# Eight weight sums and a page's sum moved from VectorE to GpSimd in the first two column groups of an encoder layer, and its third score tile issued two plain steps later

## The chip, the cores and the metric

The kernel runs on one core of a Trainium2 chip. Its engines are TensorE (PE; the loading of its stationary operand is listed as PEld), VectorE (DVE), ScalarE (ACT), GpSimd (POOL) and SyncE (SP), which here issues the DMA transfers. The metric is the device time of one execution in microseconds (us); lower is better.

## The reference, cut to what matters

One layer of an encoder over 2048 tokens of width 1024, in float32:

```python
h = rms_norm(x, norm_mix)
z = h @ w_in                       # 1024 x 4352: q_a k_a v_a q_b k_b v_b gate_a gate_b
y_a = windowed_gqa(q_a, k_a, v_a, sink)       # window 128, ALiBi, 8 heads over 2 KV heads
y_b = neighborhood_attn(q_b, k_b, v_b, rpb)   # 8 x 16 neighbourhood on a 32 x 64 grid
x = x + (sigmoid(g_a + b_a) * (y_a @ w_proj_a) + sigmoid(g_b + b_b) * (y_b @ w_proj_b)) @ w_out
x = x + square(relu(rms_norm(x, norm_mlp) @ w_up)) @ w_down
return rms_norm(x, norm_final)
```

The change touches the start of `h @ w_in` and the start of the windowed attention.

## The kernel before

**Number format.** Every large product is made of three matmuls (lines 313 to 315, and 203 to 205 in a later stage). An operand is split into a high part, rounded to the matmul format, and the rest: ScalarE casts the high part (L309) and VectorE subtracts it from the source (L310). An operand is ready for L313 when its high part is there, for L314 or L315 when the rest is.

**The first stage.** Tokens are taken in four pages of 512. The product of the first two pages with `w_in` goes by a Strassen scheme: a group of columns is cut into four quarters `a11, a12, a21, a22` (two halves of the columns, two halves of the 1024 inputs), the two token pages likewise, and seven products per group (numbers 1, 2, 5, 6, 7, 4, 3 in `ORDER`) replace eight. Products 5, 6 and 3 need sums of weight quarters first: `s1 = a21 + a22`, `a21 = a11 - a21`, `s2 = a22 - a21`, `a12 = a12 - s2`. They need sums of token pages too (`zraw` tiles t1 and t3 hold them, made from the pages `zh1`, `zh2`). `in_left` (L398) yields the weight operand of each product; `add` (L304) is the helper that makes every sum; `left_parts` splits the result into a `zwhl` tile.

**The start.** Each of the eight 128-token tiles `xin` is normalised: ScalarE and VectorE sum the squares (L236, L238), VectorE joins them (L241), GpSimd raises the result to the power -1/2 (L242), VectorE multiplies (L559 for the first page, L577 for the second), TensorE transposes (L301) into PSUM, and from PSUM ScalarE and VectorE write the scaled high part and rest (L534, L537). Column group 0 (`quad0`, weights in `kvw` tiles, 128 columns a quarter) and group 1 (`quad1`, weights in `zraw` tiles, 256 columns a quarter) run through the same stretch, and the page sum `t1 = zh1 high + zh1 rest` (two instructions of 128x1024) is made there too. The sums `s1` and `s2` of both groups share a ring of two `zS` buffers: the third `zS` waits until the split of the first is done, the fourth until that of the second is.

**What sets the order.** Python code issues the instructions, and a scheduler of the framework places them on each engine's queue; `tc.issue_after(x)` keeps an instruction behind `x` in that order. Each queue is worked off in its order, and waits on semaphores where a value comes from elsewhere (or, on GpSimd, from its own instruction just before).

**The attention's start.** `Unit.score` issues two matmuls of a score tile (L821) into one of two PSUM buffers `s`; VectorE adds the bias `biasa` and reads the tile out (L825). Between the score tiles of the first units run "plain steps", three matmuls each of the column tiles of the other two token pages. The table `FIRST` says how many plain steps precede each score tile: (0, 2), the third tile, stands at 14 and (1, 0) at 16.

Of the kernel before, what the change touches and what calls it, by code (L numbers as in the profile page):

```python
# [8 lines left out]
F32 = mybir.dt.float32  # L9
F32R = mybir.dt.float32r  # L10
AF = mybir.ActivationFunctionType
ALU = mybir.AluOpType
# [10 lines left out]
P = 128  # L23
# [72 lines left out]
def encoder_layer(ctx, tc, x, norm_mix, w_in, b_gate, sink, rpb, w_pa, w_pb, w_out,  # L96
# [41 lines left out]
    power = cr.tile([P, 1], F32, name="power")  # L138
# [83 lines left out]
            if k < KC - 1:  # L222
                yield "step"

    last_dma = [None]

    def load_tile(pl, tag, bufs, rows):
        t = T(pl, [P, D], F32, tag, bufs)
# [3 lines left out]
    def rstd_shared(pl, t):  # L232

        st = T(pl, [P, 4], F32, "st", 4)
        junk = T(pl, [P, 512], F32, "junk", 1)
        A.activation(junk, t[:, 0:512], AF.Square, accum_out=st[:, 0:1])  # L236
        other = T(pl, [P, 512], F32, "junkv", 1)
        V.tensor_tensor_reduce(out=other, in0=t[:, 512:1024], in1=t[:, 512:1024], scale=1.0, scalar=0.0,  # L238
                               op0=ALU.mult, op1=ALU.add, accum_out=st[:, 1:2])
        r = st[:, 2 : 3]  # L240
        V.scalar_tensor_tensor(out=r, in0=st[:, 0:1], scalar=D * EPS, in1=st[:, 1:2], op0=ALU.add, op1=ALU.add)  # L241
        G.tensor_tensor(out=r, in0=r, in1=power, op=ALU.pow)  # L242
        return r

    def rstd_of(pl, t, jp=None, mean=False):
# [57 lines left out]
    def add(eng, out, a, b, op=ALU.add):  # L303
        return eng.tensor_tensor(out=out, in0=a, in1=b, op=op).ins  # L304
# [90 lines left out]

    last_part, last_low = [None], [None]

    def in_left(ws, w, skip=(), behind=None):  # L398

        a11, a21 = ws[0][:, :, 0:w], ws[0][:, :, w : 2 * w]  # L400
        a12, a22 = ws[1][:, :, 0:w], ws[1][:, :, w : 2 * w]

        def parts(src, eng):
            return left_parts(src, w, eng)

        s1, s2 = None, None
        for n in ORDER:
            if n in skip:
                continue
            with tc.issue_after(behind[0]) if behind else nullcontext():  # L410
                if n == 5:
                    s1 = in_sum()[:, :, 0:w]
                    add(V, s1, a21, a22)
                elif n == 6:
                    add(V, a21, a11, a21, ALU.subtract)
                    s2 = in_sum()[:, :, 0:w]
                    add(V, s2, a22, a21, ALU.subtract)
                elif n == 3:
                    add(V, a12, a12, s2, ALU.subtract)
            yield parts({1: a11, 2: a12, 5: s1, 6: s2, 7: a21, 4: a22, 3: a12}[n], V)  # L420

    def v_parts(col, b, vt, p2, v2):
# [139 lines left out]
    for k in range(KC):  # L562
# [2 lines left out]
        h, l = (t[:, k % 4] for t in right[1 + k // 4])  # L565
        scaled(h, ps, k)
        last_low[0] = scaled_less(l, ps, k, h.bitcast(F32)).ins
    sums0, sums1 = [last_low[0]], [None]
    t1, t3 = in_raw(), in_raw()

    quad0 = in_quad(*QUADS[0], in_left(ws0, P, behind=sums0), right, xpool[1:], xpool[:1])
    quad1 = in_quad(*QUADS[1], in_left(ws1, 256, behind=sums1), right)
    next(quad0)
    next(quad0)
    sums1[0] = last_low[0]
    for n, t in enumerate(tiles[1]):
        V.tensor_scalar(t, t, rstd_shared(xp, t), float(D) ** 0.5, ALU.mult, ALU.mult)  # L577
    next(quad1)
# [9 lines left out]
    for p in range(2):  # L588
        t = T(xp, [P, D], F32, "xin", 8).rearrange("p (k c) -> p k c", k=4)
        c = QUADS[2][0]  # L590
        SY.dma_start(t, w_in[0][p * BT : (p + 1) * BT, c : c + 256].rearrange("(k p) f -> p k f", p=P))
        ops2.append(left_parts(t, 256, V))
        if p == 0:
            with tc.issue_after(last_part[0]):
                for o, h, l in zip(halves(t1), *map(halves, right[1])):
                    add(V, o, h.bitcast(F32), l.bitcast(F32))
        next(quad2)
    for n in (5, 3, 6):
        right[n] = (in_page[n](), in_page[n]())
# [309 lines left out]
        load_kv(g, 0)  # L909
    units = [Unit(g, i) for g in (1, 0) for i in range(7)] + [Unit(g, i) for g in range(2) for i in range(7, 16)]  # L910
    AHEAD, PLAIN, SCORE, STEP = 3, 24 * KC, 0.27, 0.68
    FIRST = {(0, 2): 14, (1, 0): 16, (1, 2): 18, (2, 0): 20, (2, 2): 22, (3, 0): 24}

    def prepare(n):
        if n + 2 < len(units):
# [853 lines left out]
```

## Time and profile before

| what | value |
|---|---|
| median of 3 runs | 2587.47 us (2585.76 to 2590.54) |
| the profiled execution's own time | 2589.41 us |
| its span | 2587.6 us, 34569 instructions |
| granted TensorE clock, mean | 0.999 |
| GpSimd (POOL) | 366.9 us busy (14%), 493 instructions |
| GpSimd between 28 and 66 us | 0 us busy |
| DMA over the span | 189 GB/s |

The page gives for each engine the busy time within one profiled execution. Rows of the timeline read: start and length in us, engine, line, operation, output and inputs, shape, count; in brackets the idle time of the engine before it and what ended that. In the profile VectorE's row at 26.20 us, for example, is the split L310 of a 128x1024 weight tile. A row that joins several instructions ("x4") shows the length of all of them.

### The profile page before, as it was taken

How to read it: one execution, taken by the hardware profiler on the slowest of the kernel's cores; microseconds unless marked ns; L12 is line 12 of the kernel's file. 1: busy time of each engine (PE TensorE's matmuls, PEld its weight loads, DVE VectorE, ACT ScalarE, POOL GpSimd, SP SyncE). 2: the span in 40 equal slices, each digit the busy share in tenths (PEclk: the TensorE clock that was granted, in tenths of full speed). 3: DMA queues.
4: the chain of work that ended last, by engine and by line, in shares of the span. 5: the costliest groups of instructions: out<-in, count | busy, mean ns of one | idle time of the engine just before them, and what ended most of it. 6: DMA issues, size and time to landing. Idle time of an engine off the chain costs nothing.

```text
span 2587.6 us, 34569 instructions
## 1 busy us (share of the span) xinstructions
PE 2562.3 (99%) x12140; PEld 2142.1 (83%) x12140; DVE 1608.8 (62%) x2621; ACT 1234.9 (48%) x2261; POOL 366.9 (14%) x493
## 2 busy tenths in 40 slices
PE   8999999999999999999999999999999999999999
PEld 6888778888888888888888888888888888888887
DVE  8866656765544444665578767866666535554766
ACT  5334347776565556443335554654454322323454
POOL 1000024455555541000000000100000000000010
PEclk9999999999999999999999999999999999999999
DMA  5657486476967646775456666844428835445555
GB/s 186 205 155 208 124 253 182 126 191 186 232 190 196 190 138 227 230 220 167 134 179 230 232 210 212 305 162 164 153 101 314 281 100 183 144 154 163 187 195 172
DMA packets 354126, 490.39 MB, mean 190 GB/s; under 512 B 28808, under 2 KB 188808, under 8 KB 351776
## 3 DMA queue, kind: packets, MB, share of 16 engines
q1 hardware_dynamic: 346896, 471.14, 58.6%
q10 hardware_dynamic: 7056, 17.04, 1.8%
q8 instruction: 96, 1.57, 0.3%
q14 instruction: 78, 0.64, 0.1%
HBM read 328.64 MB, written 159.45 MB: 189 GB/s over the span
## 4 chain that ended last, share of the span: by engine, by line
PE 94%; DVE 3%; DMA 2%; ACT 1%; issue 1%; SPq 0%; POOL 0%; POOLq 0%; DVEq 0%; ACTq 0%
PE b L313 16%; PE b L315 16%; PE b L314 16%; PE mm L205 6%; PE mm L203 6%; PE mm L204 6%; PE zb L313 3%; PE zb L315 3%; PE zb L314 3%; PE pt L203 2%; PE pt L204 2%; PE pt L205 2%; PE av L1088 2%; PE pt L1067 2%; PE s L1036 2%; PE pt L843 2%
## 5 line engine op out<-in xcount | busy, mean ns | idle before, releaser
L314 PE MATMUL b<-dwh,dah 128*128 128x512 f32 x896 | 348.5, 389 | 0.0
L315 PE MATMUL b<-dwh,dah 128*128 128x512 f32 x896 | 347.6, 389 | 0.0
L313 PE MATMUL b<-dwh,dah 128*128 128x512 f32 x896 | 339.6, 389 | 0.0
L309 ACT CAST dah<-da 128x1024 fp32r<-128x1024 f32 (+1 forms) x128 | 120.9, 945 | 368.9 <-PE b L315 241.8
L310 DVE TENSOR_TENSOR dah<-da,dah 128x1024 fp32r<-128x1024 f32 (+1 forms) x128 | 139.4, 1089 | 222.6 <-ACT dah L309 218.3
L314 PE MATMUL b<-ubh,uwhlb 128*128 128x512 f32 x592 | 230.3, 389 | 0.0
L313 PE MATMUL b<-ubh,uwhlb 128*128 128x512 f32 x592 | 230.2, 389 | 0.0
L315 PE MATMUL b<-ubh,uwhlb 128*128 128x512 f32 x592 | 229.2, 389 | 0.0
L203 PE MATMUL mm<-hT,whl 128*128 128x512 f32 x544 | 217.9, 401 | 0.4 <-DVE zc L304 0.4
L205 PE MATMUL mm<-hT,whl 128*128 128x512 f32 x544 | 213.5, 393 | 0.0
L204 PE MATMUL mm<-hT,whl 128*128 128x512 f32 x544 | 213.0, 391 | 0.0
L314 PEld LDWEIGHTS b<-dwh,dah 128*128 128x128 f32 x896 | 168.2, 188 | 35.0
L315 PEld LDWEIGHTS b<-dwh,dah 128*128 128x128 f32 x896 | 168.2, 188 | 34.9
L313 PEld LDWEIGHTS b<-dwh,dah 128*128 128x128 f32 x896 | 168.2, 188 | 34.9
L313 PE MATMUL zb<-zh,zwhl 128*128 128x512 f32 x476 | 186.5, 394 | 6.1 <-DVE st L253 2.0
L314 PE MATMUL zb<-zh,zwhl 128*128 128x512 f32 x476 | 186.5, 392 | 0.0
L315 PE MATMUL zb<-zh,zwhl 128*128 128x512 f32 x476 | 183.5, 391 | 1.8 <-DVE zwhl L310 1.8
L304 DVE TENSOR_TENSOR uc<-b,uc 128x512 f32<-128x512 f32 x160 | 109.0, 688 | 103.3 <-PE b L315 102.4
L1639 POOL TENSOR_TENSOR st<-st,power 128x1 f32<-128x1 f32 x16 | 13.4, 843 | 925.2 <-DVE st L1638 925.2
L313 PEld LDWEIGHTS b<-ubh,uwhlb 128*128 128x128 f32 x592 | 111.1, 188 | 23.4 <-issue 0.4
L314 PEld LDWEIGHTS b<-ubh,uwhlb 128*128 128x128 f32 x592 | 111.1, 188 | 23.2
L315 PEld LDWEIGHTS b<-ubh,uwhlb 128*128 128x128 f32 x592 | 111.1, 188 | 23.0
(262 smaller groups left out, 5839.5 us busy)
## 6 DMA issues: line engine op xcount, KB each, us to landing
at<-uc SPq DMA_DIRECT2D x224, 256.0 KB
da<-at SPq DMA_DIRECT2D x96, 512.0 KB
dw<-in_w_down_dram SPq DMA_DIRECT2D x160, 256.0 KB
uraw<-in_w_up_dram SPq DMA_DIRECT2D x32, 1024.0 KB
raw<-in_w_in_dram SPq DMA_DIRECT2D x34, 512.0 KB
zraw<-in_w_in_dram SPq DMA_DIRECT2D x16, 1024.0 KB
z<-zg SPq DMA_DIRECT2D x64, 256.0 KB
zg<-zc SPq DMA_DIRECT2D x32, 256.0 KB
```

What stands on the lines that cost most here:

```text
L203: PE.matmul(ps, lh, rh, start=first, stop=False)
L204: PE.matmul(ps, lh, rl, start=False, stop=False)
L205: return PE.matmul(ps, ll, rh, start=False, stop=last).ins
L304: return eng.tensor_tensor(out=out, in0=a, in1=b, op=op).ins
L309: casts.append(A.copy(hi, src).ins)
L310: return eng.tensor_tensor(out=lo, in0=src, in1=hi.bitcast(F32), op=ALU.subtract).ins
L313: PE.matmul(ps, lh, rh, start=first, stop=False, skip_group_check=True)
L314: PE.matmul(ps, lh, rl, start=False, stop=False, skip_group_check=True)
L315: PE.matmul(ps, ll, rh, start=False, stop=last, skip_group_check=True)
L843: ins = PE.transpose(pt[:, u * P : (u + 1) * P], self.s[:, u, c * P : (c + 1) * P], ident).ins
L1036: ins = PE.matmul(ps[:, :n], self.q[:, i, :], kv[:, z, B_R0[i] // 4 : (B_R0[i] + B_NR[i]) // 4, 4 * B_C0[j] : 4 * (B_C0[j] + w)], start=z ...
L1067: ins = PE.transpose(pt[:kp, at + (i - i0) * P : at + (i - i0 + 1) * P], self.s[i][:, rr : rr + kp], ident).ins
```

## The change

Three things are edited. `in_left` takes an engine for its sums, and both first groups pass GpSimd (`eng=G`); the other groups keep VectorE. The two halves of the page sum t1 go to GpSimd. The marks that held these sums back in the order are replaced: the sums of group 0 are held back by nothing, `s1` of group 1 and the page sum stand behind the last power (`last_root`). In the table `FIRST`, (0, 2) goes from 14 to 16 and (1, 0) from 16 to 17.

```diff
-    last_dma = [None]
+    last_dma, last_root = [None], [None]
...
-        G.tensor_tensor(out=r, in0=r, in1=power, op=ALU.pow)
+        last_root[0] = G.tensor_tensor(out=r, in0=r, in1=power, op=ALU.pow).ins
...
-    def in_left(ws, w, skip=(), behind=None):
+    def in_left(ws, w, skip=(), eng=V, behind=None):
...
-            with tc.issue_after(behind[0]) if behind else nullcontext():
-                if n == 5:
-                    s1 = in_sum()[:, :, 0:w]
-                    add(V, s1, a21, a22)
-                elif n == 6:
-                    add(V, a21, a11, a21, ALU.subtract)
-                    s2 = in_sum()[:, :, 0:w]
-                    add(V, s2, a22, a21, ALU.subtract)
-                elif n == 3:
-                    add(V, a12, a12, s2, ALU.subtract)
+            if n == 5:
+                s1 = in_sum()[:, :, 0:w]
+                with tc.issue_after(behind[0]) if behind else nullcontext():
+                    add(eng, s1, a21, a22)
+            elif n == 6:
+                add(eng, a21, a11, a21, ALU.subtract)
+                s2 = in_sum()[:, :, 0:w]
+                add(eng, s2, a22, a21, ALU.subtract)
+            elif n == 3:
+                add(eng, a12, a12, s2, ALU.subtract)
...
-    sums0, sums1 = [last_low[0]], [None]
...
-    quad0 = in_quad(*QUADS[0], in_left(ws0, P, behind=sums0), right, xpool[1:], xpool[:1])
-    quad1 = in_quad(*QUADS[1], in_left(ws1, 256, behind=sums1), right)
+    quad0 = in_quad(*QUADS[0], in_left(ws0, P, eng=G), right, xpool[1:], xpool[:1])
+    quad1 = in_quad(*QUADS[1], in_left(ws1, 256, eng=G, behind=last_root), right)
...
-            with tc.issue_after(last_part[0]):
+            with tc.issue_after(last_root[0]):
                 for o, h, l in zip(halves(t1), *map(halves, right[1])):
-                    add(V, o, h.bitcast(F32), l.bitcast(F32))
+                    add(G, o, h.bitcast(F32), l.bitcast(F32))
...
-    FIRST = {(0, 2): 14, (1, 0): 16, (1, 2): 18, (2, 0): 20, (2, 2): 22, (3, 0): 24}
+    FIRST = {(0, 2): 16, (1, 0): 17, (1, 2): 18, (2, 0): 20, (2, 2): 22, (3, 0): 24}
```

Lines behind the edit move up by two (L577 becomes L575, L821 becomes L819). The edit moves more than the sums, since the scheduler places the other instructions anew.

**GpSimd's queue at the second page's powers, before** (`st` is a tile's sum of squares; the last row belongs to a stage far behind):

```order
L242 TENSOR_TENSOR st_235<-st_235,power 128x1
L242 TENSOR_TENSOR st_343<-st_343,power 128x1
L242 TENSOR_TENSOR st_351<-st_351,power 128x1
L242 TENSOR_TENSOR st_359<-st_359,power 128x1
L242 TENSOR_TENSOR st_367<-st_367,power 128x1
L255 TENSOR_TENSOR st_1756<-st_1756,power 128x1
```

**and with the change** (`zraw_303` is the page sum t1; `zraw_197`, `zraw_207` are group 1's weights, `kvw_193`, `kvw_195` group 0's):

```order
L242 TENSOR_TENSOR st_343<-st_343,power 128x1
L242 TENSOR_TENSOR st_351<-st_351,power 128x1
L242 TENSOR_TENSOR st_359<-st_359,power 128x1
L242 TENSOR_TENSOR st_367<-st_367,power 128x1
L304 TENSOR_TENSOR zraw_303<-zh_25_243,zh_26_244 128x1024 x2
L304 TENSOR_TENSOR zS_624<-zraw_197,zraw_207 128x1024
L304 TENSOR_TENSOR zraw_197<-zraw_197 128x4x256
L304 TENSOR_TENSOR zS_664<-kvw_195,kvw_193 128x4x128
L304 TENSOR_TENSOR kvw_195<-kvw_195,zS_664 128x4x128
L304 TENSOR_TENSOR zS_685<-zraw_207,zraw_197 128x1024
L304 TENSOR_TENSOR zraw_207<-zraw_207,zS_685 128x4x256
```

Eight sums (the page sum is two) now follow the last power; the other two, `zS_606` and `kvw_193`, stand ahead of these four powers, behind those of the first page. The first three follow each other without a wait on another engine; `zS_664` waits for VectorE's split of `zS_606`, and `zS_685` for that of `zS_624` (the ring of two); `zraw_197`, `kvw_195` and the last `zraw_207` each wait for the instruction ahead of them.

**VectorE's queue where the second page's last tile, `xin_205`, is multiplied by its power, before:**

```order
L310 TENSOR_TENSOR zwhl_408<-zraw_207,zwhl_408 128x1024
L460 SCALAR_TENSOR_TENSOR ze_338<-zb_308,ze_338 128x512
L304 TENSOR_TENSOR zS_624<-zraw_197,zraw_207 128x1024
L577 TENSOR_SCALAR xin_205<-xin_205,st_367 128x1024
L310 TENSOR_TENSOR zwhl_447<-xin_445,zwhl_447 128x1024
L304 TENSOR_TENSOR zraw_303<-zh_25_243,zh_26_244 128x1024 x2
L304 TENSOR_TENSOR zraw_197<-zraw_197 128x4x256
L310 TENSOR_TENSOR zwhl_484<-xin_482,zwhl_484 128x1024
L537 SCALAR_TENSOR_TENSOR zraw_303<-zb_527,g_mix,zraw_303 128x512
```

**and with the change:**

```order
L310 TENSOR_TENSOR zwhl_408<-zraw_207,zwhl_408 128x1024
L575 TENSOR_SCALAR xin_205<-xin_205,st_367 128x1024
L460 SCALAR_TENSOR_TENSOR ze_338<-zb_308,ze_338 128x512
L310 TENSOR_TENSOR zwhl_447<-xin_445,zwhl_447 128x1024
L537 SCALAR_TENSOR_TENSOR zraw_303<-zb_527,g_mix,zraw_303 128x512
L537 SCALAR_TENSOR_TENSOR zraw_303<-zb_534,g_mix,zraw_303 128x512
L537 SCALAR_TENSOR_TENSOR zraw_303<-zb_541,g_mix,zraw_303 128x512
L537 SCALAR_TENSOR_TENSOR zraw_303<-zb_548,g_mix,zraw_303 128x512
L310 TENSOR_TENSOR zh_62_522<-zraw_303,zh_61_521 128x1024
```

Four 128x1024 sums have left this piece, the multiply of `xin_205` now stands ahead of L460, and the split `zwhl_484` now follows the four L537, a split of t1 and six more L537, eleven instructions later than before. On TensorE the six transposes of `xin_205` moved ahead of the matmuls that wait for L460.

**VectorE's queue at `zwhl_626`, the split of group 1's first sum, which TensorE's product 5 of group 1 needs, before:**

```order
L304 TENSOR_TENSOR zS_664<-kvw_195,kvw_193 128x4x128
L310 TENSOR_TENSOR zh_66_526<-zraw_303,zh_65_525 128x1024
L537 SCALAR_TENSOR_TENSOR zraw_303<-zb_577,g_mix,zraw_303 128x512
L537 SCALAR_TENSOR_TENSOR zraw_304<-zb_577,g_mix,zraw_304 128x512
L537 SCALAR_TENSOR_TENSOR zh_64_524<-zb_577,g_mix,zh_63_523 128x512
L537 SCALAR_TENSOR_TENSOR zraw_303<-zb_586,g_mix,zraw_303 128x512
L537 SCALAR_TENSOR_TENSOR zraw_304<-zb_586,g_mix,zraw_304 128x512
L537 SCALAR_TENSOR_TENSOR zh_64_524<-zb_586,g_mix,zh_63_523 128x512
L310 TENSOR_TENSOR zwhl_626<-zS_624,zwhl_626 128x1024
```

**and with the change:**

```order
L537 SCALAR_TENSOR_TENSOR zraw_304<-zb_586,g_mix,zraw_304 128x512
L537 SCALAR_TENSOR_TENSOR zh_64_524<-zb_586,g_mix,zh_63_523 128x512
L310 TENSOR_TENSOR zh_68_603<-zraw_304,zh_67_602 128x1024
L304 TENSOR_TENSOR zraw_303<-zh_27_245,zraw_303 128x1024
L310 TENSOR_TENSOR zh_66_526<-zraw_303,zh_65_525 128x1024
L310 TENSOR_TENSOR zh_68_603<-zraw_304,zh_67_602 128x1024
L304 TENSOR_TENSOR zraw_303<-zraw_303,zh_28_246 128x1024
L310 TENSOR_TENSOR zwhl_626<-zS_624,zwhl_626 128x1024
```

Five instructions of 128x1024 that stood behind this split now stand ahead of it.

At the attention's start, TensorE's third and fourth score tiles move behind the six matmuls of plain steps 15 and 16, and the fifth and sixth follow three matmuls later. Score tiles 7 onward and all plain steps keep their places. On GpSimd one weight split of 128x1024 (L180) there moves ahead of the four instructions that scale unit 0's shares (L836).

More of the change, by code (lines that the diff above doesn't have):

```diff
@@ L567, in encoder_layer @@
         last_low[0] = scaled_less(l, ps, k, h.bitcast(F32)).ins
-    sums0, sums1 = [last_low[0]], [None]
     t1, t3 = in_raw(), in_raw()
-    quad0 = in_quad(*QUADS[0], in_left(ws0, P, behind=sums0), right, xpool[1:], xpool[:1])
-    quad1 = in_quad(*QUADS[1], in_left(ws1, 256, behind=sums1), right)
+    quad0 = in_quad(*QUADS[0], in_left(ws0, P, eng=G), right, xpool[1:], xpool[:1])
+    quad1 = in_quad(*QUADS[1], in_left(ws1, 256, eng=G, behind=last_root), right)
     next(quad0)
     next(quad0)
-    sums1[0] = last_low[0]
     for n, t in enumerate(tiles[1]):
```

## The prediction

> **What bounds the kernel now.** I read the page first, then TensorE's waits (engine, line <- what it waited for: total us, times, longest), then the busy times by stretch (length; PE, PEld, DVE, ACT, POOL with counts; granted clock; DMA).
>
> ```profile
> PE 2562.3 (99%) x12140; PEld 2142.1 (83%) x12140; DVE 1608.8 (62%) x2621; ACT 1234.9 (48%) x2261; POOL 366.9 (14%) x493
> ...
> PE zb L315 <- DVE zwhl L310: 1.8, 2, 1.4
> PE zb L313 <- DVE zh L537: 1.6, 1, 1.6
> PE zb L313 <- DVE ze L460: 1.3, 2, 0.9
> PE s L821 <- DVE sta L825: 1.1, 1, 1.1
> ...
> 32.00:52.00 20.00, 18.05 (x83) 14.48 (x82) 20.00 (x28) 15.73 (x24) 0.00 (x0) 1.00 0.19 53
> 52.00:66.00 14.00, 12.24 (x52) 9.49 (x53) 14.00 (x15) 4.52 (x6) 0.00 (x0) 1.00 0.52 150
> ```
>
> TensorE is busy all but 25 us of the span, so little can be won anywhere. In the stretch of the change VectorE is busy in every microsecond while GpSimd does nothing, and TensorE waits for VectorE for 1.8 + 1.6 + 1.3 = 4.7 us. The third score tile waits 1.1 us. All the change can win is thus about 5.8 us. What it can lose shows in the row at which TensorE last waits in this stretch:
>
> ```profile
> 28.07 0.50 PE L313 MATMUL zb<-zh,zwhl 128*128 128x512 f32 x1 [0.93 <-DVE ze L460]
> ...
> 53.02 0.50 PE L315 MATMUL zb<-zh,zwhl 128*128 128x512 f32 x1 [0.34 <-DVE zwhl L310]
> ...
> 63.83 0.39 PE L314 MATMUL zb<-zh,zwhl 128*128 128x512 f32 x1
> 65.64 0.50 PE L315 MATMUL zb<-zh,zwhl 128*128 128x512 f32 x1 [1.42 <-DVE zwhl L310]
> ```
>
> At 53.02 TensorE gets `zwhl_626`, 48 matmuls (one per 0.23 us) bring it to 64.1, and from 65.64 on it runs without a wait of any size to 265 us. I measure by that second L315: it can issue 11.04 us after the first, unless its own split is late.
>
> **The terms: VectorE without any hindrance.**
>
> ```profile
> 26.20 1.22 DVE L310 TENSOR_TENSOR zwhl<-zraw,zwhl 128x1024 fp32r<-128x1024 f32 x1
> 27.34 0.68 DVE L460 SCALAR_TENSOR_TENSOR ze<-zb,ze 128x512 fp32r<-128x512 f32 x1
> 27.94 1.21 DVE L304 TENSOR_TENSOR zS<-zraw,zraw 128x1024 f32<-128x1024 f32 x1
> ...
> 24.64 1.57 DVE L577 TENSOR_SCALAR xin<-xin,st 128x1024 f32<-128x1024 f32 x2
> ...
> 30.87 2.35 DVE L304 TENSOR_TENSOR zraw<-zh,zh 128x1024 f32<-128x1024 f32 x2
> ...
> 35.41 2.72 DVE L537 SCALAR_TENSOR_TENSOR zraw<-zb,g_mix,zraw 128x512 f32<-128x512 f32 x4
> 38.05 0.68 DVE L460 SCALAR_TENSOR_TENSOR ze<-zb,ze 128x512 fp32r<-128x512 f32 x1
> ...
> 51.75 1.21 DVE L310 TENSOR_TENSOR zwhl<-zS,zwhl 128x1024 fp32r<-128x1024 f32 x1
> ...
> 43.73 1.05 ACT L309 CAST zh<-zraw 128x1024 fp32r<-128x1024 f32 x1 [1.28 <-DVE zraw L537]
> ...
> 26.43 1.40 POOL L242 TENSOR_TENSOR st<-st,power 128x1 f32<-128x1 f32 x1 [1.00 <-DVE st L241]
> ```
>
> From start to start VectorE takes 1.13 us for a split or sum of 128x1024, 0.66 for an L537 and about that for an L577 (0.73 at most), 0.60 for a 128x512. Removed are six sums at 1.13 and four at 0.60, 9.2 us; none lies beside idle VectorE time. Two small ones (1.2 us) stood ahead of the last power. Since the same two on GpSimd can push a split of group 0 back by up to 1.2 us (they start when the second `kvw` tile lands at 12.4 us, between two splits that start at 12.33 and 13.1), I leave the last power where it is: its end is 26.43 + 1.40 = 27.83, bounds 1.2 us either way.
>
> From there to the end of `zwhl_626` the new order has, in this row: L575 0.66, L460 0.60, L310 1.13, four L537 2.64, L310 1.13, six L537 3.96, two L310 2.27, L460 0.60, L310 1.13, L460 0.60, a half L310 0.60, six L537 3.96, six of 128x1024 6.78: 26.06. One of the last six needs ScalarE's cast of a page part that VectorE wrote just before: 1.05 more. That ends at 54.94, where it ended at 52.96 before. So even unhindered, the relief of 9.2 us is spent: the five page parts put ahead of `zwhl_626` (5.65 us) and the splits drawn in behind the power eat it. The split waits for nothing that comes late on GpSimd, yet L537 number 3 needs the second page-sum half, 4.8 us behind the power, which costs 1.1 us: 56.0, the second L315 at 67.1, +1.5 us.
>
> **GpSimd's price, and the hindrance.** Sums on GpSimd have one near row, its weight splits:
>
> ```profile
> L180 POOL TENSOR_TENSOR whl<-raw,whl 128x1024 fp32r<-128x1024 f32 x32 | 76.9, 2403 | 61.6 <-ACT whl L179 59.9 <-PE pt L843 1.7
> ...
> 1348.21 4.62 DVE L304 TENSOR_TENSOR uraw<-uraw,uraw 128x1024 f32<-128x1024 f32 x4
> ...
> 1348.44 4.80 POOL L255 TENSOR_TENSOR st<-st,power 128x1 f32<-128x1 f32 x1 [15.16 <-DVE st L253]
> ...
> 375.87 0.16 DVE L833 TENSOR_TENSOR sta<-sta 128x4 f32<-128x4 f32 x1 [0.45 <-ACT sa L832]
> ...
> 556.21 0.37 DVE L833 TENSOR_TENSOR sta<-sta 128x4 f32<-128x4 f32 x1 [2.58 <-ACT sa L832]
> ...
> 554.16 2.40 POOL L180 TENSOR_TENSOR whl<-raw,whl 128x1024 fp32r<-128x1024 f32 x1
> ...
> 571.97 0.71 DVE L833 TENSOR_TENSOR sta<-sta 128x4 f32<-128x4 f32 x1 [1.94 <-ACT sa L832]
> ...
> 571.11 1.00 POOL L836 TENSOR_SCALAR sa<-sa,sta 128x288 f32<-128x288 f32 x2
> 572.04 0.63 POOL L803 CAST qa<-qraw 128x512 fp32r<-128x512 f32 x1
> ```
>
> A 128x1024 sum costs 2.40 us there, twice VectorE's, and a half one by its size 1.2. The rows above tell what happens where both engines read two operands from SBUF. A power, otherwise 0.55 to 0.93 us, took 4.80 because four sums ran back to back on VectorE; it ended 0.4 behind them. A 0.16 us VectorE sum starting at 556.21 ended at 556.58, just behind GpSimd's split (556.56). The one at 571.97 ended at 572.68, behind two GpSimd instructions in a row (572.67), not behind the first (572.11). So one excludes the other for a whole instruction, and a holder with its next instruction ready keeps on. L537, L460 and the like read one operand from PSUM and run free.
>
> With the change three sums (two page halves, `zS_624`) stand ready behind the last power, which is also what L575 on `xin_205` waits for; GpSimd's next instruction starts within the end of its last (572.04 against 572.11), VectorE's follows a semaphore. I take GpSimd as first. Kept for three sums, L575 starts at 27.83 + 7.2 = 35.03; behind it in VectorE's queue are L460, which frees the PSUM bank for TensorE's L313 (28.07 before), and all else. L575 and L460 end at 36.3; the fourth sum, which must wait for the third, takes 35.7 to 38.1, so the next L310 loses 1.8. From 38.1 remain 24.8 + 1.05: `zwhl_626` at 63.95, the second L315 at 75.05, **+9.4 us**. Sums five and six run under six L537 and cost nothing; `zS_685` waits for `zwhl_626` and then takes 2.4 + 1.05 + 1.13 and VectorE's rows between, some 10 us, inside the 11.04. Were the lock given back after each sum, L575 would lose 2.4, the next L310 1.8, the one behind four L537 2.2: `zwhl_626` at 61.3, +6.8 us.
>
> The Trainium skill, "SBUF — State Buffer", § Who interferes with whom, states this lock, and names `tensor_scalar` in a two-port mode as taking the pair too; no row here shows an L577 waiting behind GpSimd. If L575 did not wait, the first loss would fall on the next L310 instead, and the sum would be about 2.4 us less.
>
> **The clock.** TensorE now idles for some 8 us around 28 to 36 and some 5 us ahead of the first L315. What follows a gap here:
>
> ```profile
> 262.92 0.39 PE L315 MATMUL zb<-zh,zwhl 128*128 128x512 f32 x1
> 265.27 0.47 PE L313 MATMUL zb<-zh,zwhl 128*128 128x512 f32 x1 [1.97 <-DVE st L253]
> ...
> 266.48 0.63 PE L314 MATMUL zb<-zh,zwhl 128*128 128x512 f32 x1
> ...
> 266.00:268.00 2.00, 2.00 (x6) 1.56 (x6) 1.25 (x4) 1.94 (x2) 0.00 (x0) 0.51 0.44 169
> ```
>
> After 1.97 us idle the granted clock fell to 0.51, and eight matmuls took 0.43 us instead of 0.23: 1.6 us. After the gaps of 1.4 and 1.6 us at 52 and 65.6 it did not. Behind the first gap the loss is hidden, since VectorE's split comes later; behind the second it is on the path. Bounds 0 and 1.6; I take half, **+0.8**. The Trainium skill, "TensorE: Matmul & The Clock Gate", Part 1, has the clock halved only after an idle window of about 3.4 us; this trace shows it after less. By either, a 5 us gap would pay it whole, an estimate of +0.8 more.
>
> **The third score tile.**
>
> ```profile
> 370.95 0.51 POOL L763 TENSOR_SCALAR biasa<-biasa,byhead 128x288 f32<-128x288 f32 x1 [8.75 <-DMA biasa<-in_dist_a_dram]
> ...
> 371.50 0.38 DVE L825 CUSTOM_DVE_ANT_0 sa<-s,biasa,byhead 128x160 f32<-128x160 f32 x1 [10.45 <-POOL biasa L763]
> ...
> 371.94 0.84 PE L821 MATMUL s<-ka,qa 128*128 128x224 f32 x4 [1.10 <-DVE sta L825]
> ...
> 381.62 0.60 PE L843 MATMUL pt<-ident,sa 128*128 128x128 f32 x4
> ```
>
> It waits for a PSUM buffer until VectorE, held by the bias, has read the first tile out at 371.9. Six matmuls more in front (1.37 us) cover the whole 1.10: **-1.1**, at worst 0. Unit 0's shares now stand behind a 2.4 us split on GpSimd; by my placing they end near 378.6, and their reader (381.62, now about 380.5) does not notice.
>
> **Sum:** 9.4 + 0.8 - 1.1 = +9.1 us, or 6.5 with the lock given back each time. The profiled execution took 2589.41, 1.8 outside its span; against it the sum is 2598.5. It was slower than the median of the three runs, 2587.47, to which I add: **2596.6 us**.
>
> **Rivals.**
> 1. *No exclusion that matters* (VectorE's instruction gets in first, GpSimd fills the gaps): +1.5 for the row above, -1.1, and 0 to 1.6 for the clock: 2588 to 2589.5, no change to tell. For it: GpSimd's powers mostly yielded to VectorE. Against: 571.97. Chance 0.20.
> 2. *The relief lands, faster.* The place is `zwhl_626`: it decides for a gain when that split ends before TensorE arrives, about 49.5 us; then the 4.7 and the 1.1 vanish, 2581.7. It would need 26 us of VectorE work from 27.83 done in 22. Chance 0.06.
> 3. *The score tile does not gain* (its bias lands two steps later too, the transfer being queued behind others): 1.1 on top of any case; against it, the transfer keeps its place in SP's queue. Chance 0.1 within the others.
> 4. *Worse than a lock:* GpSimd slower on these shapes, or late sums holding `zwhl_687`: 2600 to 2606. Chance 0.06.
>
> **The numbers.** The forecast, exclusion in either form, has 0.68 (three sums kept 0.4, one at a time 0.28), with its own range 2592 to 2599.5. Rivals take the rest. What can be told from no change is 0.2%, 5.2 us. Slower by more: 0.68 + 0.06 and nothing from rival 1, 0.74; same 0.20; faster 0.06. The gap at 265 us, hung on arriving transfers, can shift by its own 3.6 us. The range, 2588.0 to 2600.5, leaves out the half of rival 1 below, rival 2, and most of rival 4.
>
> **What would show it.** Right: the L575 on `xin_205` starting or lasting to about 35 (one at a time: 30); TensorE's wait ahead of its transposes near 7 us; the first L315 of product 5 near 64; a stretch of clock near 0.5 behind it; later matmuls shifted alike, less 1.1 behind 372. Wrong: an L575 done by 29 and VectorE's two-operand instructions at 1.2 us beside GpSimd's sums, or GpSimd's sums stretched instead, which would mean VectorE goes first.

## The result, and the profile after

The changed kernel takes 2595.32 us (median of 12 runs, 2592.72 to 2596.85), the kernel before 2590.32 us in the same series (12 runs); the ratio is 1.0023 with a 95% interval of 1.0015 to 1.003, so 4 to 8 us slower. The profiled execution took 2596.24 us, its span 2594.3, 6.7 us more than the span before.

The first line of the page after, and TensorE's waits in the first 400 us (engine, line <- what it waited for: total us, times, longest):

```profile
PE 2566.1 (99%) x12140; PEld 2145.3 (83%) x12140; DVE 1608.9 (62%) x2611; ACT 1235.6 (48%) x2261; POOL 389.9 (15%) x503
...
PE zb L313 <- DVE ze L460: 4.1, 1, 4.1
PE zb L301 <- DVE xin L575: 3.6, 1, 3.6
PE zb L313 <- DVE zc L304: 2.6, 2, 2.4
```

VectorE has ten instructions fewer and is busy as long as before (1608.8 us): what was taken off it came back as time in which it was kept waiting inside its instructions. TensorE is busy 3.8 us longer with the same 12140 matmuls, and the stretches below show why: some run at half clock. The other 2.9 us of the 6.7 are more idle time.

The timeline of VectorE and of GpSimd behind the last power shows the exchange (start, length, engine, line, operation, output<-inputs, shape, count):

```profile
27.67 2.83 DVE L575 TENSOR_SCALAR xin<-xin,st 128x1024 f32<-128x1024 f32 x1 [0.44 <-POOL st L242]
30.41 0.68 DVE L460 SCALAR_TENSOR_TENSOR ze<-zb,ze 128x512 fp32r<-128x512 f32 x1
31.02 2.79 DVE L310 TENSOR_TENSOR zwhl<-xin,zwhl 128x1024 fp32r<-128x1024 f32 x1
33.73 2.71 DVE L537 SCALAR_TENSOR_TENSOR zraw<-zb,g_mix,zraw 128x512 f32<-128x512 f32 x4
36.37 3.25 DVE L310 TENSOR_TENSOR zh<-zraw,zh 128x1024 fp32r<-128x1024 f32 x1
...
45.96 0.68 DVE L460 SCALAR_TENSOR_TENSOR ze<-zb,ze 128x512 fp32r<-128x512 f32 x1
```

```profile
27.61 5.12 POOL L304 TENSOR_TENSOR zraw<-zh,zh 128x1024 f32<-128x1024 f32 x2
32.69 3.38 POOL L304 TENSOR_TENSOR zS<-zraw,zraw 128x1024 f32<-128x1024 f32 x1
36.15 2.40 POOL L304 TENSOR_TENSOR zraw<-zraw 128x1024 f32<-128x1024 f32 x1
```

L575, 0.75 us long elsewhere, takes 2.83; the next split 2.79 instead of 1.22, the one behind four L537 3.25. Each ends about its own length behind the end of one GpSimd sum: 33.81 against 27.61 + 5.12 = 32.73, and 39.62 against 38.55. GpSimd's third sum in turn is 3.38 long instead of 2.40, since it had to let the split, which ends at 33.81, finish first. L460 and L537, which read from PSUM, keep their 0.68 and 0.66 us beside it all.

TensorE's timeline, and behind it one stretch of the busy times (length; PE, PEld, DVE, ACT, POOL with counts; granted clock; DMA):

```profile
42.17 0.39 PE L315 MATMUL zb<-zh,zwhl 128*128 128x512 f32 x1
46.70 0.79 PE L313 MATMUL zb<-zh,zwhl 128*128 128x512 f32 x1 [4.13 <-DVE ze L460]
...
51.13 0.63 PE L314 MATMUL zb<-zh,zwhl 128*128 128x512 f32 x1
...
60.97 0.39 PE L315 MATMUL zb<-zh,zwhl 128*128 128x512 f32 x1
...
71.85 0.39 PE L315 MATMUL zb<-zh,zwhl 128*128 128x512 f32 x1
...
378.38 0.62 PE L819 MATMUL s<-ka,qa 128*128 128x224 f32 x4
```

```profile
47.00:52.00 5.00, 5.00 (x13) 3.90 (x13) 5.00 (x8) 0.00 (x0) 2.57 (x2) 0.52 0.72 197
```

The wait that decides is at 46.70: 4.13 us for L460, which stands behind all three held instructions. Then ten matmuls run at half clock, one per 0.43 us instead of 0.23. (The wait of 3.6 us ahead of the transposes at 30.55 has eight such matmuls behind it too, but the one at 46.70 ends later and hides it.) The first L315 of group 1's product 5 at 60.97 and the second at 71.85 (65.64 before, +6.2) wait for nothing. The third score tile at 378.38 waits for nothing either.

Later stretches nearly cancel in this pair of profiles. The wait at 265 us before (1.97 us, and its half clock) is 0.63 us here; at 354.40 us stands one of 2.42 us, with eight matmuls at half clock, where before it was 0.23 + 0.39. Both hang on arriving transfers: behind the first stands ScalarE's L250, behind the second its L179, and each waits for a DMA. The first comes out anywhere from 0.18 to 2.84 us in the thirteen profiles of this document, the second from 0.17 to 2.42, in kernels with and without the change, so I do not count them to it.

### The profile page after: what moved, and what is told of

The parts are those of the page before. It is cut to its first block, busy times and chain, and to the rows that moved or that the text cites. A ratio compares the mean times of both kernels' runs of the same rounds, so it can differ in the third digit from the quotient of the medians.

```text
span 2594.3 us, 34564 instructions
## 1 busy us (share of the span) xinstructions
PE 2566.1 (99%) x12140; PEld 2145.3 (83%) x12140; DVE 1608.9 (62%) x2611; ACT 1235.6 (48%) x2261; POOL 389.9 (15%) x503
## 3 DMA queue, kind: packets, MB, share of 16 engines
q10 hardware_dynamic: 7056, 17.04, 1.8%
q8 instruction: 95, 1.56, 0.3%
## 4 chain that ended last, share of the span: by engine, by line
PE 92%; DMA 3%; DVE 2%; ACT 1%; issue 1%; SPq 1%; POOL 0%; POOLq 0%; DVEq 0%; ACTq 0%
PE b L313 16%; PE b L314 16%; PE b L315 16%; PE mm L205 6%; PE mm L203 6%; PE mm L204 6%; PE zb L313 3%; PE zb L315 3%; PE zb L314 3%; PE pt L203 2%; PE pt L204 2%; PE pt L205 2%; PE av L1086 2%; PE pt L1065 2%; PE s L1034 2%; PE pt L841 2%
## 5 line engine op out<-in xcount | busy, mean ns | idle before, releaser
L315 PE MATMUL b<-dwh,dah 128*128 128x512 f32 x896 | 347.6, 389 | 0.0
L313 PE MATMUL b<-dwh,dah 128*128 128x512 f32 x896 | 339.6, 389 | 0.0
L310 DVE TENSOR_TENSOR dah<-da,dah 128x1024 fp32r<-128x1024 f32 (+1 forms) x128 | 139.6, 1091 | 222.4 <-ACT dah L309 222.4
L313 PE MATMUL b<-ubh,uwhlb 128*128 128x512 f32 x592 | 230.2, 389 | 0.0
L315 PE MATMUL b<-ubh,uwhlb 128*128 128x512 f32 x592 | 229.2, 389 | 0.0
L313 PEld LDWEIGHTS b<-dwh,dah 128*128 128x128 f32 x896 | 168.2, 188 | 35.0
L315 PEld LDWEIGHTS b<-dwh,dah 128*128 128x128 f32 x896 | 168.2, 188 | 34.9
L313 PE MATMUL zb<-zh,zwhl 128*128 128x512 f32 x476 | 188.5, 397 | 8.0 <-DVE ze L460 4.1
L315 PE MATMUL zb<-zh,zwhl 128*128 128x512 f32 x476 | 184.9, 394 | 0.0
L313 PEld LDWEIGHTS b<-ubh,uwhlb 128*128 128x128 f32 x592 | 111.1, 188 | 23.5 <-issue 0.4
L315 PEld LDWEIGHTS b<-ubh,uwhlb 128*128 128x128 f32 x592 | 111.1, 188 | 23.0
```

The lines of the kernel that those rows point to most:

```text
L310: return eng.tensor_tensor(out=lo, in0=src, in1=hi.bitcast(F32), op=ALU.subtract).ins
L313: PE.matmul(ps, lh, rh, start=first, stop=False, skip_group_check=True)
L315: PE.matmul(ps, ll, rh, start=False, stop=last, skip_group_check=True)
```

## The experiments

Theory A throughout: GpSimd's sums hold back VectorE's instructions that have all their operands in SBUF. All ratios are against the kernel before in the same series; each kernel ran eleven times, the sums alone five times, the change with L460 first seven times. The last column is of one profiled execution. L575, L460 and L537 carry other line numbers where an edit adds lines.

| kernel | median us | before | ratio, 95% interval | second L315, us |
|---|---|---|---|---|
| table alone | 2587.58 | 2588.24 | 0.9996 (0.9987 to 1.0005) | 66.08 |
| sums alone | 2598.21 | 2588.24 | 1.0038 (1.0024 to 1.0051) | 73.76 |
| sums in halves | 2591.92 | 2588.24 | 1.0015 (1.0006 to 1.0024) | 69.03 |
| no sums at all | 2587.91 | 2588.24 | 1.0000 (0.9992 to 1.0009) | 65.67 |
| all sums behind the power | 2592.24 | 2588.44 | 1.0011 (1.0002 to 1.0020) | 69.64 |
| late pair only | 2586.86 | 2588.44 | 0.9989 (0.9980 to 0.9998) | 64.77 |
| no sums, L460 first | 2585.82 | 2588.44 | 0.9990 (0.9981 to 0.9998) | 63.55 |
| the change, L460 first | 2596.70 | 2588.44 | 1.0028 (1.0017 to 1.0039) | 71.62 |
| behind the power, in halves | 2591.47 | 2588.54 | 1.0010 (1.0001 to 1.0020) | 69.14 |
| without group 0's sums | 2593.91 | 2588.54 | 1.0018 (1.0010 to 1.0027) | 71.44 |
| gated by a buffer | 2589.41 | 2588.54 | 1.0003 (0.9994 to 1.0012) | 66.03 |

### The two parts apart

The kernel before with the table's edit:

```diff
-    FIRST = {(0, 2): 14, (1, 0): 16,
+    FIRST = {(0, 2): 16, (1, 0): 17,
```

> The kernel before with only the table's two entries changed, (0, 2) at 16 and (1, 0) at 17; all sums stay on VectorE. Theory A (the exclusion between GpSimd and VectorE explains the loss, the score tile gains): the 1.10 us wait ahead of the third score tile is gone and the time is 1.1 to 1.7 us below the kernel before, ratio about 0.9995. Rival C (the later score tile brings a new wait, or the bias lands later too): no gain, 0 to 2 us above the kernel before.

And the change with the old table:

```diff
-    FIRST = {(0, 2): 16, (1, 0): 17,
+    FIRST = {(0, 2): 14, (1, 0): 16,
```

> The change without the table's edit: all ten sums on GpSimd, score tiles at 14 and 16 as before. Theory A: 1.1 to 1.7 us above the changed kernel, so some 6 to 8 us above the kernel before, ratio 1.0025 to 1.003; the waits of 3.6 and 4.1 us in the first 50 us stay. Rival C: the time is below the changed kernel's.

The wait behaves as theory A has it; the time of the first kernel is not clear of no change. In the first kernel no wait is left ahead of the score tile; in the second it is there, longer than before:

```profile
379.15 0.37 PE L819 MATMUL s<-ka,qa 128*128 128x224 f32 x1 [2.16 <-DVE sta L823]
```

So the edit covers a wait of 1.1 us in one execution and of 2.2 in another. It does not always cover all of it: in two kernels below that have the edit, 0.48 us (sums in halves) and 1.2 us (the change, L460 first) of the wait are left. The times say 1 us (2588.24 to 2587.58) and, against the changed kernel's ratio, 3.9 (1.0038 to 1.0023), with intervals of 2 us and more; a finer number stays open, the more so as the second L315 already stands 1.9 us later here than in the changed kernel (73.76 against 71.85), for a reason that the early pair shows below. The sums alone cost 10 us, 6 to 13 by the interval, where 6 to 8 were expected.

### Nothing on GpSimd, the same order on VectorE

The ten sums are left out; VectorE's remaining instructions stand in the changed kernel's order.

```diff
-                s1 = in_sum()[:, :, 0:w]
-                    add(eng, s1, a21, a22)
+                    s1 = a21
...
-                for o, h, l in zip(halves(t1), *map(halves, right[1])):
-                    add(G, o, h.bitcast(F32), l.bitcast(F32))
```

> The changed kernel with the ten sums left out altogether (a quarter or a page part as it stands takes the sum's place), so neither GpSimd nor VectorE makes them; VectorE's order of what remains is the changed kernel's. Theory A: the waits at 30 and 46 us shrink to below 1.5 us each, the second L315 of group 1 starts at 65 to 67 us (65.64 before, 71.85 with the change), and the time is near that of the kernel before, -3 to +1 us, since the order alone gives the relief back. Rival B: the second L315 stays near 71 us and the time 4 to 6 us above the kernel before. Rival 2 of the prediction (the relief would land): the waits vanish, 4 us or more below the kernel before.

VectorE's and TensorE's rows of this kernel:

```profile
27.54 0.75 DVE L580 TENSOR_SCALAR xin<-xin,st 128x1024 f32<-128x1024 f32 x1 [0.44 <-POOL st L242]
28.21 0.68 DVE L465 SCALAR_TENSOR_TENSOR ze<-zb,ze 128x512 fp32r<-128x512 f32 x1
28.81 1.21 DVE L310 TENSOR_TENSOR zwhl<-xin,zwhl 128x1024 fp32r<-128x1024 f32 x1
...
40.81 0.68 DVE L465 SCALAR_TENSOR_TENSOR ze<-zb,ze 128x512 fp32r<-128x512 f32 x1
...
41.55 0.50 PE L313 MATMUL zb<-zh,zwhl 128*128 128x512 f32 x1 [2.05 <-DVE ze L465]
...
53.37 1.22 DVE L310 TENSOR_TENSOR zwhl<-zraw,zwhl 128x1024 fp32r<-128x1024 f32 x1
...
54.64 0.50 PE L315 MATMUL zb<-zh,zwhl 128*128 128x512 f32 x1 [0.97 <-DVE zwhl L310]
...
65.67 0.39 PE L315 MATMUL zb<-zh,zwhl 128*128 128x512 f32 x1
```

Two things follow. First, the holds are real and sized: the L460 that decides starts at 40.81 here and at 45.96 in the changed kernel, 5.15 us apart, in the same order of instructions; VectorE's busy time is 1599.5 us against 1608.9. Nor is it the wait for a sum's result, which this kernel leaves out too: in the changed kernel none of VectorE's rows between L575 and this L460 has a gap that GpSimd ends. Secondly, even with the sums free VectorE's relief brings nothing: the second L315 stands where it stood before (65.67 against 65.64), and the new order, which puts L460 behind six L537 and `zwhl_626` behind five page parts, is the likely reason; the section on the order tests it. One figure of the expectation missed: the wait at 41.55 us is 2.05, not below 1.5.

### Half as long a hold

```diff
+        for o, x, y in zip(halves(out), halves(a), halves(b)):
+            add(eng, o, x, y, op)
...
+                for j in range(4):
+                    add(G, t1[:, j], right[1][0][:, j].bitcast(F32), right[1][1][:, j].bitcast(F32))
```

> The changed kernel with each 128x1024 sum on GpSimd made as two instructions of 128x512; VectorE's order is the same. Theory A, given back after each instruction: L575 on xin_205 and the two next splits wait about 1.2 us less each, the wait ahead of L313 at 46.7 comes near 43 us, and the time is 2 to 4 us below the changed kernel's. Rival A2 (GpSimd keeps VectorE out while its next instruction is ready): L575 waits for all four halves, no gain. Rival B (VectorE's new order, not the exclusion, is the cause): the time is the changed kernel's within 1 us.

VectorE's rows of this kernel, and GpSimd's row of the four halves:

```profile
29.13 1.75 DVE L581 TENSOR_SCALAR xin<-xin,st 128x1024 f32<-128x1024 f32 x1 [0.44 <-POOL st L242]
30.80 0.68 DVE L466 SCALAR_TENSOR_TENSOR ze<-zb,ze 128x512 fp32r<-128x512 f32 x1
31.40 1.70 DVE L310 TENSOR_TENSOR zwhl<-xin,zwhl 128x1024 fp32r<-128x1024 f32 x1
33.03 2.06 DVE L543 SCALAR_TENSOR_TENSOR zraw<-zb,g_mix,zraw 128x512 f32<-128x512 f32 x3
...
36.21 1.62 DVE L310 TENSOR_TENSOR zh<-zraw,zh 128x1024 fp32r<-128x1024 f32 x1
...
44.16 0.68 DVE L466 SCALAR_TENSOR_TENSOR ze<-zb,ze 128x512 fp32r<-128x512 f32 x1
...
29.07 6.43 POOL L304 TENSOR_TENSOR zraw<-zh,zh 128x512 f32<-128x512 f32 x4
```

L575 takes 1.75 us instead of 2.83, the splits 1.70 and 1.62 instead of 2.79 and 3.25. With four halves ready in a row L575 waited for one. A hold thus lasts as long as GpSimd's one instruction, and rival A2 (GpSimd keeps on while it has more) falls. B fell with the kernel without sums, which has the same order. From the start of L575 to the start of the L460 that decides it is 15.03 us here and 18.29 in the changed kernel; since L575 itself starts 1.46 us later in this profile, the wait ends at 44.90 and not near 43 as expected. By the ratios 2 us are won, though by the intervals alone it could also be nothing.

### Group 0's early pair

In the changed kernel `zS_606` and the first `kvw` sum run on GpSimd at 12 us. Here they stand behind the last power:

```diff
-    quad0 = in_quad(*QUADS[0], in_left(ws0, P, eng=G), right, xpool[1:], xpool[:1])
+    quad0 = in_quad(*QUADS[0], in_left(ws0, P, eng=G, behind=last_root), right, xpool[1:], xpool[:1])
```

> The changed kernel with group 0's first two sums on GpSimd held behind the last power as well; VectorE's order is the changed kernel's. Theory A (each GpSimd sum that stands ready holds the next two-operand instruction of VectorE back once): the two splits at 12.3 us take 1.46 us together again and TensorE's wait at 15 us is below 0.4 us, but GpSimd's row behind the power is two sums (2.6 us) longer, so one or two more splits of VectorE near 36 to 42 us wait 1 to 2 us each. The second L315 of group 1 stays at 71 to 73 us, the time within 1.5 us of the changed kernel's. Rival D (the early pair is the larger part of the loss): 2 us or more below the changed kernel's.

The gain by the ratios is 3 us (the intervals leave room for none), so the expectation (within 1.5) missed, and the number is the one that rival D gives. What the early pair does is plain in the kernel with the sums alone: VectorE's two splits, 1.46 us together before, become 3.43.

```profile
12.37 3.43 DVE L310 TENSOR_TENSOR zwhl<-kvw,zwhl 128x512 fp32r<-128x512 f32 x2
...
12.19 1.39 POOL L304 TENSOR_TENSOR zS<-kvw,kvw 128x512 f32<-128x512 f32 x1 [0.53 <-DMA kvw<-in_w_in_dram]
13.66 1.60 POOL L304 TENSOR_TENSOR kvw<-kvw 128x512 f32<-128x512 f32 x1
```

Whether it is 0.8 us (the changed kernel's profile) or 2 us (three other kernels with the early pair) hangs on which engine comes first, within some tenths of a microsecond: the first split starts at 11.92 in the changed kernel, ahead of GpSimd's first sum at 12.30, and at 12.37 here, behind the one at 12.19. Between the profile of the changed kernel and that with all sums behind the power this is not where the gain lies, since L575 starts at 27.67 in the one and at 27.71 in the other. And rival D falls by the next kernel, in which group 0's four sums are left out:

```diff
-    quad0 = in_quad(*QUADS[0], in_left(ws0, P, eng=G), right, xpool[1:], xpool[:1])
+    quad0 = in_quad(*QUADS[0], in_left(ws0, P, eng=None), right, xpool[1:], xpool[:1])
```

> The changed kernel with the four sums of group 0 left out (quarters as they stand take their place), so that only the page sum and group 1's sums remain on GpSimd; VectorE's order is the changed kernel's. Theory A: no hold at 12.3 us, but L575 on xin_205 and the next two splits still wait for the three sums behind the power (2.8, 2.8 and about 3.2 us long), the wait ahead of L313 stays at 2.9 to 4.2 us, and the time is 2 to 4 us above the kernel before. Rival D (group 0's early pair is the larger part): the time is within 1 us of the kernel without any sums.

1.0018 (1.0010 at the least), where D had within 1 us of the kernel without sums: most of the loss stays with the page sum and group 1's sums alone. The test is not quite clean, since with the ring free GpSimd makes its last two sums earlier, and they hold one split more (1.73 us at 43.06).

The kernel with all sums behind the power seems to do better than this one, though their intervals overlap. The first two rows are of that kernel, the last three of this one:

```profile
36.41 2.02 DVE L310 TENSOR_TENSOR zh<-zraw,zh 128x1024 fp32r<-128x1024 f32 x1
...
45.49 0.50 PE L313 MATMUL zb<-zh,zwhl 128*128 128x512 f32 x1 [2.90 <-DVE ze L460]
```

```profile
35.74 3.26 DVE L310 TENSOR_TENSOR zh<-zraw,zh 128x1024 fp32r<-128x1024 f32 x1
...
43.06 1.73 DVE L310 TENSOR_TENSOR zwhl<-xin,zwhl 128x1024 fp32r<-128x1024 f32 x1
...
46.59 0.79 PE L313 MATMUL zb<-zh,zwhl 128*128 128x512 f32 x1 [4.67 <-DVE ze L463]
```

Of the 1.80 us between their second L315, 1.10 are there at the end of this wait: GpSimd's shorter sums fall elsewhere, and a split takes 2.02 us instead of 3.26. The other 0.70 come behind it: the gap of 4.67 us is followed by matmuls at half clock, the one of 2.90 us is not. The mean clock of their executions points the same way: 0.997 or 0.998 in all eleven without group 0's sums, 0.998 or 0.999 in the other eleven. Against the changed kernel the same two parts are 1.21 and 1.00 us, of 2.21.

Both cures together, the pair behind the power and halves:

> The changed kernel with both cures at once: group 0's first pair behind the last power, and each 128x1024 sum on GpSimd in two instructions of 128x512; all ten sums stay on GpSimd and VectorE's order is the changed kernel's. Theory A (the loss is the holds, and they add up): the two gains of 2 and 3 us add, second L315 of group 1 at 67 to 68.5 us, time 0 to 2 us above the kernel before, ratio about 1.0003, near that of the kernel without the sums. Rival: the two cures take away the same loss, ratio stays at 1.001 or above.

They do not add up (1.0010). More instructions on GpSimd behind the power reach two splits more, at 39.94 and 41.79 us. From L575's start to that of the L460 that decides it is 16.80 us here, 17.04 with all sums behind the power in one piece, 15.03 with halves alone, and 13.27 without sums: halving the holds hardly lessens their sum when there are more to meet.

### The order

The L537 of page 2's second half are held behind L460, as they stood before; this also puts three page parts behind `zwhl_626`. Once without the sums, once in the changed kernel:

```diff
-            scaled_less(t1[:, kk], ps, k, t1[:, kk])
+            with tc.issue_after(last_low[0]):
+                scaled_less(t1[:, kk], ps, k, t1[:, kk])
```

> The kernel without the ten sums, with one order more: the L537 of the second half of page 2 are held behind L460 of group 1, as they stood before, which also puts three of the five page parts behind zwhl_626. Theory A with the prediction's reading (the new order gives VectorE's relief back): the wait at 41.55 us shrinks below 0.8 us and the one ahead of the first L315 vanishes; the second L315 starts at 62 to 63.5 us against 65.7, and the time is 3 to 5 us below the kernel before. Rival B2 (the row is bound by the transposes and ScalarE, whatever the order): the time is that of the kernel without the sums, within 1 us of the kernel before.

> The changed kernel, all ten sums on GpSimd, with the same one order more. Theory A: L575 and the next splits wait for GpSimd as in the changed kernel (2.8 us each), but L460 comes some 4 us earlier, the wait of 4.1 us at 46.7 falls below 1.5 us, no stretch at half clock follows it, the second L315 starts at 66 to 69 us, and the time is 3 to 5 us below the changed kernel's. Rival: the wait moves to zwhl_626 or to the transposes, no gain over 1 us.

Without the sums the second L315 comes at 63.55 instead of 65.67, and the time falls by 2.6 us: the order does give back part of the relief (a wait of 1.56 us ahead of the first L315 stayed, so the row and the time gained less than expected). In the changed kernel the same order wins nothing, and the expectation failed: L460 is on time, but GpSimd's later sums now meet splits and page sums instead of L537, and TensorE's waits move to the splits (1.62 us at 57.64 and 1.38 at 68.21), as the rival had it.

```profile
58.10 3.95 DVE L310 TENSOR_TENSOR zh<-zraw,zh 128x1024 fp32r<-128x1024 f32 x2
61.97 3.41 DVE L304 TENSOR_TENSOR zraw<-zh,zraw 128x1024 f32<-128x1024 f32 x1
```

### Sums where nothing collides

In the changed kernel `zS_664` and the second `kvw` sum cost nothing: they wait for a split of VectorE that stands right ahead of six L537, and run beside these. So only this pair goes to GpSimd, with the table's edit:

```diff
-                    add(V, s2, a22, a21, ALU.subtract)
+                    add(eng, s2, a22, a21, ALU.subtract)
...
-                    add(V, a12, a12, s2, ALU.subtract)
+                    add(eng, a12, a12, s2, ALU.subtract)
...
-    quad0 = in_quad(*QUADS[0], in_left(ws0, P, behind=sums0), right, xpool[1:], xpool[:1])
+    quad0 = in_quad(*QUADS[0], in_left(ws0, P, behind=sums0, eng=G), right, xpool[1:], xpool[:1])
```

> The kernel before with the table's edit and only two sums on GpSimd, s2 and a12 of group 0 (zS_664, kvw_195), which cannot start before VectorE's split of zS_606 and so run beside L537; VectorE's order is that of before without these two. Theory A: no two-operand instruction of VectorE is longer than 1.3 us between 26 and 66 us because of them, 1.2 us of VectorE's row is saved, the wait at 52 us shrinks from 1.55 to below 0.6 us, and the time is 2 to 3 us below the kernel before, ratio about 0.999. Rival: GpSimd's two sums run into a split, no gain beyond the score tile's 1.1 us.

```profile
41.46 1.29 POOL L304 TENSOR_TENSOR zS<-kvw,kvw 128x512 f32<-128x512 f32 x1 [13.31 <-DVE zwhl L310]
42.84 1.29 POOL L304 TENSOR_TENSOR kvw<-kvw,zS 128x512 f32<-128x512 f32 x1
...
41.30 1.40 DVE L537 SCALAR_TENSOR_TENSOR zraw<-zb,g_mix,zraw 128x512 f32<-128x512 f32 x2
42.62 0.74 DVE L537 SCALAR_TENSOR_TENSOR zh<-zb,g_mix,zh 128x512 fp32r<-128x512 f32 x1
43.28 1.40 DVE L537 SCALAR_TENSOR_TENSOR zraw<-zb,g_mix,zraw 128x512 f32<-128x512 f32 x2
```

GpSimd's two sums in these rows and VectorE's L537 all keep their lengths, the wait at 52 us falls from 1.55 to 0.95 (below 0.6 was expected), and the kernel is faster than the changed one and the kernel before: 0.9989, 0.5 to 5 us below the latter. How much of it is the table and how much the pair, these intervals don't tell.

A last kernel tried the same with group 1's first two sums, by giving `zS_624` the buffer of `zS_606`, so that it too must wait for that split:

```diff
-    in_sum = ring(s_z, "zS", [P, 4, 256], F32, 2)
+    in_sums = [ring(s_z, f"zS{n}", [P, 4, 256], F32, 1) for n in range(2)]
...
-                    s1 = in_sum()[:, :, 0:w]
+                    s1 = in_sums[0]()[:, :, 0:w]
...
-                    s2 = in_sum()[:, :, 0:w]
+                    s2 = in_sums[0 if w == P else 1]()[:, :, 0:w]
```

> The kernel before with the table's edit and four sums on GpSimd that a buffer makes wait for a split of VectorE: s1 and a21 of group 1 (zS and zraw, 128x1024) cannot start before the split of group 0's first sum, which stands right ahead of six L537, and s2 and a12 of group 0 not before the split of group 1's first; the page sum and the rest stay on VectorE. Theory A: nothing stands ready behind the last power, so L575 takes 0.75 us and no two-operand instruction between 26 and 45 us is longer than 1.3 us; VectorE is 3.4 us lighter; of TensorE's 4.6 us of waits in the first 66 us half go, and the time is 2 to 5 us below the kernel before, ratio 0.998 to 0.999. Rival: the splits behind the six L537 wait for GpSimd's second sum, and group 1's split for its first: no gain beyond the score tile's.

The large sums were hidden up to a remainder of 1 us (two splits of 3.31 instead of 2.35), but the scheduler's order put the small pair beside a sum and a page part, each 1.1 us longer; TensorE's waits moved to L456 (1.31 us at 53.41) and no gain is left.

## Why the prediction was right, and where it was not

- **The sign and the cause** were right: exclusion between the two engines' SBUF operands, more than the relief is worth. L575 on `xin_205` shows it (2.83 us against 0.75), L460 and L537 stay free, and the kernel without sums loses nothing with the order unchanged.
- **The step "kept for three sums, L575 starts at 35.03"** failed. Each time one GpSimd instruction went by, not three. I had weighed 571.97 against, one row of a short sum, and let it stand for a rule. Of the two forms that I priced, the other held, to which I had given the smaller chance. For it I had losses of 2.4, 1.8 and 2.2 us; the three instructions took 2.08, 1.57 and 2.03 more than their own lengths. I had `zwhl_626` end at 61.3 and the second L315 at 72.4 (+6.8); the split ended at 58.52 + 1.22 = 59.74, the L315 stood at 71.85 (+6.2). That 6.8 and 6.2 lie so close is in part luck, since the 6.2 has 2.0 of half clock in it, which I counted apart.

```profile
58.52 1.22 DVE L310 TENSOR_TENSOR zwhl<-zS,zwhl 128x1024 fp32r<-128x1024 f32 x1
```

- **The place.** I looked for the wait ahead of L315, on `zwhl_626`. It came ahead of L313, on L460: the order's piece that I counted through has both L460 behind six L537, and I had not asked when TensorE wants them. I had some 8 us of idling around 28 to 36 and some 5 ahead of the first L315; it was 3.60 at 30.55, 4.13 ahead of L313 and nothing ahead of the L315. The sum survives because both waits end with the same row of VectorE.
- **The clock** was mis-sized: +0.8 taken, with a bound of 1.6. Ten matmuls at 0.43 instead of 0.23 us are 2.0. So +6.2 is 5.15 of holds, plus 2.0, minus the 0.97 that the wait ahead of the first L315 would have cost anyway, plus 0.0 for the order.
- **Unhindered, +1.5:** 1.1 of it was a wait for the page sum, which the kernel without sums leaves out. Without that wait I had `zwhl_626` end at 54.94, and it ended at 53.37 + 1.22 = 54.59; the second L315 came out at +0.0 where +0.4 was left. That the relief is eaten by the order was right.
- **The early pair**, left at "up to 1.2 us either way", costs 0.8 to 2 us at VectorE's splits, and in the executions with 2 us the last power came later too (27.64 + 1.46 = 29.10 with the sums in halves, 27.83 before): a loss at the splits in every profile that has it, a gain in none.
- **The third score tile:** its wait is gone in the changed kernel, as forecast at -1.1; in two others with the same table a part of it is left.

The forecast was +9.1 us, the ratio gives +5.9 (3.9 to 7.8): too much by the second point. With the form that held, the same sum was 6.5. As a time the forecast, 2596.6, lies only 1.3 us above the measured 2595.32, and that is luck: I had added the sum to 2587.47, and the kernel before came out at 2590.32 in the series with the change.

The Trainium skill, "SBUF — State Buffer", § Who interferes with whom, says that a VectorE instruction with two SBUF inputs, or one in a two-port mode, and GpSimd shut each other out for a whole instruction. The trace agrees on both kinds: L310 2.79 us, and L575, which has one SBUF tile and the 128x1 power as inputs, 2.83.

## What to carry to other kernels

Before an elementwise operation goes from a full VectorE to an idle GpSimd, ask what VectorE does in the very 2.4 us that it takes there: beside instructions that read PSUM it is free, beside instructions that read and write SBUF alone it costs each of them up to its whole length. An operation that a semaphore or a buffer makes start at a run of PSUM reads can be moved, as the late pair was; ones that merely stood ready started at the worst place here. Then look at the order that the scheduler makes of the lighter queue, for it may spend what was won before TensorE sees it.

## What the runs showed of the hardware that I had not expected

**Turns.** With both engines loaded, they mostly took turns, one instruction each, even where GpSimd had its next sum ready (the four halves above). In one place GpSimd did not get its turn: its small sum at 54.26 us in the changed kernel with L460 first took 4.48 us, past three splits of VectorE in a row, as the power at 1348 us did past four sums. Both were GpSimd's first after more than 14 us of idling; whether that is the reason stays open.

```profile
54.26 4.48 POOL L304 TENSOR_TENSOR zS<-kvw,kvw 128x512 f32<-128x512 f32 x1 [14.33 <-DVE zwhl L310]
```

**The clock.** Over the thirteen profiles, all five gaps of TensorE between 3.6 and 4.7 us behind the first 20 us were followed by matmuls at half clock. Of shorter ones, two of 17 between 1.3 and 1.9 us were, and eight of 14 between 1.9 and 3.0: the share grows with the length, and what decides a single case these traces do not show. 1.53 and 1.57 us were enough, 2.77 and 2.90 were not. The first row below is the stretch behind a gap of 1.57 us at 52.42 (the table alone), the second the one behind a gap of 2.90 us at 45.49 (all sums behind the power).

```profile
52.00:58.00 6.00, 5.24 (x15) 3.88 (x16) 6.00 (x9) 1.47 (x2) 0.00 (x0) 0.72 0.16 33
```

```profile
46.00:52.00 6.00, 6.00 (x28) 4.92 (x28) 6.00 (x10) 2.15 (x3) 2.59 (x2) 1.00 0.63 175
```

What such a gap costs thus cannot be forecast from these traces to better than the 1.2 to 2.4 us of six to twelve matmuls at 0.43 instead of 0.23 us. The Trainium skill, "TensorE: Matmul & The Clock Gate", Part 1, has a free-running window of about 3.4 us that must be idle. The spread fits a window that does not start with the gap, but ten gaps shorter than it were followed by half clock, so the window need not be idle throughout.
